# Moving the rotary angles behind the second unit of v, and cutting the last output tile 384 + 128

## The chip, the cores and the metric

The kernel runs on one core of a Trainium2 chip. The metric is the device time of one execution in microseconds (us). The profile is one execution of the same program, taken by the hardware profiler; its engines are TensorE (PE, with its weight loads as PEld), VectorE (DVE), ScalarE (ACT), GpSimd (POOL) and SyncE (SP), which here only issues DMAs.

## The reference, cut to what matters

One encoder layer over 1024 tokens of width 1024. What the change touches is the projection of `a` to v, the angles of the rotary embedding, and the very end (gate, per-layer embedding, final norm):

```python
def rotary(x, positions):
    half = HEAD_DIM // 2
    inv_freq = ROPE_THETA ** (-jnp.arange(half, dtype=jnp.float32) / half)
    ang = positions.astype(jnp.float32)[:, None, :, None] * inv_freq
    cos, sin = jnp.cos(ang), jnp.sin(ang)
...
        a = rms_norm(h, g_mix[i])
        qa, ka, va, qd, kd, vd, gate_na, gate_dil = jnp.split(a @ w_in[i], split_points, axis=-1)
...
        e = rms_norm(h, g_ple[i])
        h = h + jax.nn.sigmoid(e @ w_ple_gate[i]) * (p[i] @ w_ple_proj[i])
    return rms_norm(h, g_final)
```

## The kernel before, in words

Matrices are held as pairs of float32r tiles, a high part and a low part (`split`, lines 106 to 113: ACT casts the high part, DVE or POOL subtracts it to get the low part), and each product is three matmuls (`mm3`, lines 206 to 210, so L208, L209 and L210 in the profile).

**The head.** For eight token tiles of 128 rows (`tt` 0 to 7) the kernel loads x, works out two of the 16 tiles of `p @ W_p` (`ple`), and normalizes and transposes the tile (`norm_to_act`, lines 278 to 282). The norm is a chain of small DVE instructions (L239 to L248) with two DVE instructions at its end that write `xn` (L258). TensorE then transposes `xn` in two halves of four 128x128 blocks (L275) into a PSUM tile `tp`. The pool of `tp` has two buffers, so each half of a tile needs the buffer that the same half of the tile before used. A buffer is free once ACT has cast it (L109, `act10h<-tp`) and DVE has subtracted (L110, `act10l<-tp`). Tiles 4 to 7 go into act10 (first half) and act11 (second half).

Then, in the code, come the rotary angles (lines 340 to 379): four DMAs that broadcast the positions into `pi`, one of `invf`, 20 DVE instructions on 128x256 that reduce the angle modulo 2 pi (L349 to L375, the tiles `a`, `b`, `c`, `d`), two Sin on ACT (L376, L377) and two stores of the tables into DRAM (L379, `cs_scr`). The tables are read back at the start of the q and k stage (L481).

**The v stage.** Five units of v (`v_unit`, line 381, called at line 423). A unit has four PSUM tiles `ps_v` of 48 matmuls with 256 columns, of three buffers (`ps_mm`). Each is cast by ACT and subtracted by DVE into `v_stage`, and stored by four DMAs in the first two units (`v_na`). The weights of a unit are prepared during an earlier unit. Beside it run `left_sums` (line 400), the operand sums of the next stage.

**The end.** For each token tile and each half of 512 columns TensorE multiplies by the gate weights (`ps_t`), ACT takes the sigmoid (L1412), DVE multiplies and adds (L1413, L1415), ACT squares and sums (L1417), and after the second half a chain of small DVE instructions gives the factor with which both halves of the output are scaled. The second half of the last tile is done in two pieces of 256 columns (lines 1430 to 1435), each with 24 matmuls.

**What sets the order.** Every engine takes its instructions in one fixed order. That order is made at build time by a list scheduler with its own model of the times, so instructions of the head and of the v stage are interleaved on each engine, and code that is written elsewhere changes the order around it. DMAs from SP stand in one queue in the same way.

Of the kernel before, what the change touches and what calls it, by code (L numbers as in the profile page):

```python
# [59 lines left out]
def encoder_kernel(ctx: ExitStack, tc: tile.TileContext, t: dict, out: bass.AP):  # L60
# [229 lines left out]
    def dma(dst, src):  # L290
        nc.sync.dma_start(dst.bitcast(F32) if dst.dtype == F32R else dst,
                          src.bitcast(F32) if src.dtype == F32R else src)
# [4 lines left out]
    with ExitStack() as st:  # L297
# [38 lines left out]
                ple(*job)  # L336
            norm_to_act(qp, two(xs[tt]), g, tt, xn=qp.tile([P, D], F32, name="xn", tag="nat"))


        pi = qp.tile([P, 256], I32, name="pi", tag="rt")  # L340
        for a in range(4):
            nc.sync.dma_start(pi[a * 32:(a + 1) * 32],
                              t["positions"][:, a * 256:(a + 1) * 256].broadcast_to((32, 256)))
        invf = qp.tile([P, 1], F32, name="invf", bufs=1)
        nc.sync.dma_start(invf, t["invf"])
        hpi = qp.tile([P, 1], F32, name="hpi", bufs=1)
        nc.vector.memset(hpi, float(np.pi / 2))
        r, k1, k2, ab, sn, cn = (qp.tile([P, 256], F32, name=n_, tag="rt") for n_ in "abcdef")
        nc.vector.tensor_copy(r, pi)  # L349
        nc.vector.tensor_scalar(r, r, invf, None, op0=ALU.mult)  # L350
        big = 4096.0 * TWO_PI
        nc.vector.tensor_scalar(k1, r, 1.0 / big, MAGIC, op0=ALU.mult, op1=ALU.add)
        nc.vector.tensor_scalar(k1, k1, MAGIC, None, op0=ALU.subtract)
        cp = _fixed_parts(big, [2.0 ** (8 - 7 * i) for i in range(8)])
        pp = _fixed_parts(TWO_PI, [2.0 ** (-9 - 12 * i) for i in range(3)])

        def less(k, part, dst=r):
            nc.vector.scalar_tensor_tensor(dst, k, -part, r, op0=ALU.mult, op1=ALU.add)

        for i in range(3):  # L360
            less(k1, cp[i])
        less(k1, cp[3], k2)
        nc.vector.tensor_scalar(k2, k2, 1.0 / TWO_PI, MAGIC, op0=ALU.mult, op1=ALU.add)
        nc.vector.tensor_scalar(k2, k2, MAGIC, None, op0=ALU.subtract)
        less(k2, pp[0])
        less(k1, cp[3])
        less(k2, pp[1])
        less(k1, cp[4])
        less(k1, cp[5])
        less(k2, pp[2])  # L370
        less(k1, cp[6])
        less(k1, cp[7])
        lim = float(np.nextafter(np.float32(np.pi), np.float32(0)))
        nc.vector.tensor_scalar(r, r, lim, -lim, op0=ALU.min, op1=ALU.max)
        nc.vector.scalar_tensor_tensor(ab, r, -1.0, r, op0=ALU.mult, op1=ALU.max)  # L375
        nc.scalar.activation(sn, r, AF.Sin)  # L376
        nc.scalar.activation(cn, ab, AF.Sin, bias=hpi, scale=-1.0)  # L377
        for i, src in enumerate((cn, sn)):
            nc.sync.dma_start(cs_scr[i].rearrange("a f n -> (a f) n"), src)  # L379

        def v_unit(u):
            w2 = take(2, 2)
            for tp_ in range(4):
                ps = ps_mm.tile([P, HALF], F32, name="ps_v", tag="mm")
                pv3 = ps.rearrange("p (a b) -> p a b", a=2)
                for a in range(2):
                    mm_tok(pv3[:, a, :], w2, tp_ * 2 + a)
                stg = qp.tile([P, 2, 4, P], F32R, name="v_stage", tag="nat")
                s4 = ps.rearrange("p (a h d) -> p a h d", a=2, h=4)
                split(stg[:, :, :, 0:64], stg[:, :, :, 64:128], s4)  # L390
                if u < 2:
                    for a in range(2):
                        for r in range(2):
                            dma(v_na[4 * u:4 * u + 4, :, 2 * a + r, tp_, :].rearrange("h c f -> c h f"),
                                stg[r * GW:(r + 1) * GW, a])
                    continue
                dst = v_scr[tp_ * 256:(tp_ + 1) * 256, u * HALF:(u + 1) * HALF]
                dma(dst.rearrange("(a p) c -> p a c", p=P), stg.rearrange("p a h d -> p a (h d)"))

        def left_sums(r):  # L400

# [19 lines left out]
        s1 = []  # L421
        for u in range(5):
            v_unit(u)
            if u < 4:
                s1.append(left_sums(u))
            if u == 0:
                for b in range(2):
                    dma(a_scr[b], flat2(act[1][0][b]))
# [972 lines left out]
    with ExitStack() as st:  # L1401
# [18 lines left out]
        for tt, n in tok_order():  # L1420
            c = slice(n * HALF, (n + 1) * HALF)
            pe = fp.tile([P, HALF], F32, name="pe", tag="pe")
            nc.sync.dma_start(pe, p_scr[tt * P:(tt + 1) * P, c])
            last = tt == NT - 1 and n == 1
            if last:

                hg = fp.tile([P, HALF], F32, name="hg", tag="hg", bufs=1)
                nc.gpsimd.tensor_tensor(hg, h_cols(tt, slice(0, HALF)), g[:, 0:HALF], op=ALU.mult)
                p = parts[tt, 0]
                for a in range(2):  # L1430
                    ps = ps_mm.tile([P, HALF], F32, name="ps_t", tag="mm")[:, :256]
                    mm_tok(ps, w8[4:], tt, slice(a * 256, (a + 1) * 256))
                    q = gated(tt, slice(HALF + a * 256, HALF + (a + 1) * 256), ps, pe[:, a * 256:(a + 1) * 256])
                    if a == 0:
                        nc.vector.tensor_tensor(p, p, q, op=ALU.add)
            else:
                q = gated(tt, c, tok_product(w8, tt, n), pe)
                parts[tt, n] = q
            if n == 1:
                r = rstd_of(fp, (parts[tt, 0], q))  # L1440
                for i in range(2):
                    c = slice(i * HALF, (i + 1) * HALF)
                    o = fp.tile([P, HALF], F32, name="o", tag="o")
# [105 lines left out]
```

## Time and profile before

| | |
|---|---|
| median of 3 runs | 1675.5 us (1675.15, 1675.5, 7496.38) |
| the profiled execution | 1673.03 us, span 1670.8 us |
| TensorE busy | 1571.5 us, 94% of the span |
| VectorE, ScalarE, GpSimd busy | 72%, 42%, 39% of the span |
| mean granted TensorE clock | 0.974 of 2.4 GHz |
| DMA | 279.22 MB, mean 167 GB/s |

A busy TensorE is one with a matmul in its pipeline. Matmuls overlap, so in rows of the timeline the distance from one start to the next is what a matmul costs in a stream, and the second column (its own duration) is longer than that. The granted clock is 1.00 at 2.4 GHz and 0.50 at 1.2 GHz. "[5.32 <-DVE act10l L110]" behind a row says that its engine had been idle for 5.32 us and that this instruction of DVE ended the wait.

### The profile page before, as it was taken

Reading aid. Unit: us, or ns where it says so; the run is one execution under the profiler, and the core shown is the slowest. Engines: PE = TensorE matmul, PEld = TensorE weight load, DVE = VectorE, ACT = ScalarE, POOL = GpSimd, SP = SyncE. Lnnn points to the kernel's source line nnn. Section 1 sums busy time; section 2 is a strip of 40 time slices with the busy share of each in tenths; the row PEclk is TensorE's granted clock in tenths of the full one; section 3 lists DMA queues with packets and bytes.
Section 4 is the critical chain, followed back from the end, with each engine's and each line's share of the span. In section 5 each row is a group of like instructions: output and inputs, shape, how many; then the busy total and the mean of one; then the engine's idle time right before and its main releaser. Section 6 shows DMA issues by size and latency. Waiting matters only on the chain. (4 is left out here: it accounts for less than half of the span.)

```text
span 1670.8 us, 22589 instructions
## 1 busy us (share of the span) xinstructions
PE 1571.5 (94%) x7787; PEld 1312.3 (79%) x7787; DVE 1200.9 (72%) x2081; ACT 708.4 (42%) x1327; POOL 654.0 (39%) x434
## 2 busy tenths in 40 slices
PE   8899999999999998879997899999989999999997
PEld 7899777787787877757886688888877788887886
DVE  6744799734665788645557776777778999999955
ACT  7322222216787666644334333333345333333422
POOL 0233678613333222215304677777742322225100
PEclk9999999999999999989998999999999999999999
DMA  8552455674566778556343344434467454433122
GB/s 309 169 156 103 138 161 160 208 266 165 189 197 217 230 224 275 182 189 183 139 164 126 107 140 139 145 139 146 145 222 277 156 167 161 143 111 128 43 101 70
DMA packets 115058, 279.22 MB, mean 167 GB/s; under 512 B 14240, under 2 KB 30592, under 8 KB 114432
## 3 DMA queue, kind: packets, MB, share of 16 engines
q1 hardware_dynamic: 109184, 267.29, 48.7%
q10 hardware_dynamic: 5760, 10.49, 1.7%
q8 instruction: 62, 1.02, 0.3%
q14 instruction: 52, 0.43, 0.1%
HBM read 186.61 MB, written 91.11 MB: 166 GB/s over the span
## 5 line engine op out<-in xcount | busy, mean ns | idle before, releaser
L109 ACT CAST w_hi<-w_raw 128x512 fp32r<-128x512 f32 (+2 forms) x103 | 83.7, 826 | 144.4 <-POOL w_raw L470 55.9
L110 POOL TENSOR_TENSOR w_lo<-w_raw,w_hi 128x512 fp32r<-128x512 f32 (+2 forms) x33 | 64.2, 1947 | 154.5 <-ACT w_hi L109 150.5
L110 DVE TENSOR_TENSOR f_lo<-f_raw,f_hi 128x512 fp32r<-128x512 f32 x80 | 81.7, 1039 | 52.0 <-ACT f_hi L109 51.3
L110 DVE TENSOR_TENSOR w_lo<-w_raw,w_hi 128x1024 fp32r<-128x1024 f32 (+1 forms) x70 | 85.2, 1224 | 37.7 <-ACT w_hi L109 37.5
L722 POOL TENSOR_SCALAR s_sb<-s_sb,rs 128x384 f32<-128x384 f32 x64 | 41.3, 645 | 134.1 <-DVE rs L721 88.9
L109 ACT CAST f_hi<-f_raw 128x512 fp32r<-128x512 f32 x80 | 46.1, 613 | 82.9 <-DMA f_raw<-w_up 79.7
L110 DVE TENSOR_TENSOR pt_l<-tp_p,pt_h 128x384 fp32r<-128x384 f32 (+3 forms) x120 | 65.0, 543 | 15.4 <-ACT pt_h L109 14.8
L1172 POOL TENSOR_TENSOR u_t<-u_t 128x512 f32<-128x512 f32 x45 | 53.7, 1193 | 38.0 <-ACT u_t L1171 36.8
L109 ACT CAST pt_h<-tp_p 128x384 fp32r<-128x384 f32 (+3 forms) x120 | 56.1, 467 | 24.3 <-PE tp_p L731 14.5
L628 POOL TENSOR_TENSOR k_lo<-k_lo,k_st 128x1024 fp32r<-128x1024 f32 x12 | 33.2, 2767 | 76.1 <-ACT k_st L625 54.4
L1171 ACT ACTIVATE u_t<-u_t 128x512 f32<-128x512 f32 x45 | 28.4, 631 | 74.5 <-DVE u_t L1158 74.1
L1335 DVE TENSOR_TENSOR h<-ps_d,h 128x512 f32<-128x512 f32 x84 | 54.4, 678 | 1.7 <-PE ps_d L210 1.5
L637 PE MATMUL sc<-k_st,q_st 128*128 128x384 f32 (+3 forms) x160 | 53.0, 331 | 0.2 <-DVE stats L655 0.2
L657 ACT ACTIVATE s_sb<-s_sb,stats 128x256 f32<-128x256 f32 (+2 forms) x96 | 44.8, 468 | 19.3 <-DVE stats L655 18.9
L647 ACT ACTIVATE s_sb<-s_sb,nm 128x384 f32<-128x384 f32 x64 | 39.4, 616 | 31.2 <-DVE nm L646 31.0
L110 DVE TENSOR_TENSOR f_lo<-f_t,f_hi 128x512 fp32r<-128x512 f32 x32 | 51.3, 1608 | 1.8
L208 PE MATMUL ps_b<-y_op,w_hi 128*128 128x512 f32 x96 | 39.3, 419 | 11.2 <-ACT y_op L109 8.5
L638 PE MATMUL sc<-k_lo,q_st 128*128 128x384 f32 (+3 forms) x160 | 49.5, 310 | 0.0
L1335 DVE TENSOR_TENSOR sum_t<-ps_d,sum_t 128x512 f32<-128x512 f32 x72 | 46.6, 679 | 2.3 <-PE ps_d L210 2.3
L210 PE MATMUL ps_d<-w_hi,m_op 128*128 128x512 f32 x112 | 43.6, 399 | 2.7 <-DVE m_op L110 2.7
L496 POOL TENSOR_TENSOR o<-x,c 128x512 f32<-128x512 f32 x24 | 40.6, 1707 | 11.2 <-DVE c L491 8.7
L1297 POOL TENSOR_TENSOR t_raw<-pair,w_raw 128x1024 f32<-128x1024 f32 x6 | 15.6, 2598 | 75.0 <-DVE act11l L110 30.8
(478 smaller groups left out, 5826.3 us busy)
## 6 DMA issues: line engine op xcount, KB each, us to landing
f_raw<-w_up SPq DMA_DIRECT2D x32, 512.0 KB
w_raw<-w_in SPq DMA_DIRECT2D x26, 512.0 KB
u_raw<-l_scr SPq DMA_DIRECT2D x25, 512.0 KB
qk_scr<-o SPq DMA_DIRECT2D x96, 128.0 KB
h<-l_scr SPq DMA_DIRECT2D x24, 512.0 KB
l_scr<-u_t SPq DMA_DIRECT2D x42, 256.0 KB
l_scr<-u_s SPq DMA_DIRECT2D x42, 256.0 KB
w_raw<-w_qk SPq DMA_DIRECT2D x20, 512.0 KB
```

What stands on the lines that cost most here:

```text
L109: nc.scalar.copy(hi, src)
L110: eng.tensor_tensor(lo, src, hi.bitcast(F32), op=ALU.subtract)
L208: nc.tensor.matmul(ps, sh, mh, start=first, stop=False)
L210: nc.tensor.matmul(ps, sl, mh, start=False, stop=last)
L496: nc.gpsimd.tensor_tensor(dst, x, y, op=op)
L637: pe(nc.tensor.matmul(o, qs[:, qsl], kk, start=True, stop=False))
L638: pe(nc.tensor.matmul(o, qs[:, qsl], ll, start=False, stop=True))
L647: nc.scalar.activation(s_[:, :n], s_[:, :n], AF.Exp, bias=nm, scale=1.0, accum_out=sm)
L657: nc.scalar.activation(s_[:, :n], s_[:, :n], AF.Exp, bias=nm, scale=-1.0, accum_out=sm)
L722: nc.gpsimd.tensor_scalar(pr, pr, rs, 1.0, op0=ALU.mult, op1=ALU.mult)
L1172: nc.gpsimd.tensor_tensor(c, c, c, op=ALU.mult)
L1335: nc.vector.tensor_tensor(d, ps, d, op=ALU.add)
```

## The change

The block of the angles becomes a function, called after the second unit of v instead of ahead of the first; its instructions are the same. And the last half tile is cut at 384 columns instead of at 256, so that its last piece has 128 columns.

```diff
-        pi = qp.tile([P, 256], I32, name="pi", tag="rt")
-        for a in range(4):
-            nc.sync.dma_start(pi[a * 32:(a + 1) * 32],
-                              t["positions"][:, a * 256:(a + 1) * 256].broadcast_to((32, 256)))
...
+        def angles():
+
+            pi = qp.tile([P, 256], I32, name="pi", tag="rt")
+            for a in range(4):
+                nc.sync.dma_start(pi[a * 32:(a + 1) * 32],
+                                  t["positions"][:, a * 256:(a + 1) * 256].broadcast_to((32, 256)))
...
         for u in range(5):
             v_unit(u)
+            if u == 1:
+                angles()
             if u < 4:
                 s1.append(left_sums(u))
...
-                for a in range(2):
-                    ps = ps_mm.tile([P, HALF], F32, name="ps_t", tag="mm")[:, :256]
-                    mm_tok(ps, w8[4:], tt, slice(a * 256, (a + 1) * 256))
-                    q = gated(tt, slice(HALF + a * 256, HALF + (a + 1) * 256), ps, pe[:, a * 256:(a + 1) * 256])
+                for a, b in ((0, 384), (384, HALF)):
+                    ps = ps_mm.tile([P, HALF], F32, name="ps_t", tag="mm")[:, :b - a]
+                    mm_tok(ps, w8[4:], tt, slice(a, b))
+                    q = gated(tt, slice(HALF + a, HALF + b), ps, pe[:, a:b])
```

**VectorE in the head, before.** From the norm of tile 6 (its `xn` is xn_514) to the subtraction that frees the first `tp` buffer of tile 5 (tp_478); a_613, b_614 and c_615 are tiles of the angles:

```order
L247 SCALAR_TENSOR_TENSOR nw_525<-ny_521,nv_519 128x1
L358 SCALAR_TENSOR_TENSOR a_613<-c_615,a_613 128x256
L243 TENSOR_SCALAR ny_577<-ny_577 128x1
L244 TENSOR_SCALAR nv_575<-nv_575 128x1
L248 SCALAR_TENSOR_TENSOR ny_521<-nw_525,ny_521 128x1
L358 SCALAR_TENSOR_TENSOR a_613<-b_614,a_613 128x256
L247 SCALAR_TENSOR_TENSOR nw_581<-ny_577,nv_575 128x1
L258 SCALAR_TENSOR_TENSOR xn_514<-x_492,ny_521,gain_136 128x512 x2
L358 SCALAR_TENSOR_TENSOR a_613<-c_615,a_613 128x256
L248 SCALAR_TENSOR_TENSOR ny_577<-nw_581,ny_577 128x1
L110 TENSOR_TENSOR act10l_88<-tp_478,act10h_87 128x512
```

The same place in the changed kernel, from the weights' low part w_lo_625 (second piece of the second unit) to the same subtraction:

```order
L110 TENSOR_TENSOR w_lo_625<-w_raw_622,w_hi_624 128x1024
L110 TENSOR_TENSOR act10l_88<-tp_422,act10h_87 128x512
L242 TENSOR_SCALAR ny_577<-nv_575 128x1
L247 SCALAR_TENSOR_TENSOR nw_525<-ny_521,nv_519 128x1
L110 TENSOR_TENSOR act11l_90<-tp_429,act11h_89 128x512
L110 TENSOR_TENSOR v_stage_677<-ps_v_628,v_stage_677 128x8x64
L243 TENSOR_SCALAR ny_577<-ny_577 128x1
L244 TENSOR_SCALAR nv_575<-nv_575 128x1
L248 SCALAR_TENSOR_TENSOR ny_521<-nw_525,ny_521 128x1
L247 SCALAR_TENSOR_TENSOR nw_581<-ny_577,nv_575 128x1
L258 SCALAR_TENSOR_TENSOR xn_514<-x_492,ny_521,gain_136 128x512 x2
L248 SCALAR_TENSOR_TENSOR ny_577<-nw_581,ny_577 128x1
```

The angles are gone from this stretch; the split of the first v tile (v_stage_733 comes next, then act10l_88<-tp_478) and the weights stand in it as before.

**SP's queue, now.** The four loads of `pi` stood between the loads of x for tiles 5 and 7; now they stand behind the stores of the first v tile of the second unit (v_stage_933):

```order
L291 DMA v_na_93<-v_stage_845 64x4x128 x4
L291 DMA v_na_93<-v_stage_933 64x4x128 x4
L362 DMA pi_1108<-positions 32x256 x4
L139 DMA w_raw_1171<-w_in 128x1024
L291 DMA v_na_93<-v_stage_989 64x4x128 x4
```

**VectorE, now, where the angles went.** They are in two runs, ahead of and behind the split of the third v tile of the second unit (v_stage_1045); this is the first run, and the line numbers are those of the changed file (349 became 369, 358 became 378):

```order
L110 TENSOR_TENSOR v_stage_989<-ps_v_940,v_stage_989 128x8x64
L369 CAST a_1117<-pi_1108 128x256
L370 TENSOR_SCALAR a_1117<-a_1117,invf_1113 128x256
L372 TENSOR_SCALAR b_1118<-a_1117 128x256
L373 TENSOR_SCALAR b_1118<-b_1118 128x256
L378 SCALAR_TENSOR_TENSOR a_1117<-b_1118,a_1117 128x256 x3
L378 SCALAR_TENSOR_TENSOR c_1119<-b_1118,a_1117 128x256
L383 TENSOR_SCALAR c_1119<-c_1119 128x256
L384 TENSOR_SCALAR c_1119<-c_1119 128x256
L378 SCALAR_TENSOR_TENSOR a_1117<-c_1119,a_1117 128x256
L110 TENSOR_TENSOR v_stage_1045<-ps_v_996,v_stage_1045 128x8x64
```

All eleven instructions of this run wait for the loads of `pi`, and v_stage_1045 stands behind them.

## Rows read from the trace of the kernel before

**Rows 1.** The page's part 1: busy us, share of the span and instructions of each engine.

```profile
PE 1571.5 (94%) x7787; PEld 1312.3 (79%) x7787; DVE 1200.9 (72%) x2081; ACT 708.4 (42%) x1327; POOL 654.0 (39%) x434
```

**Rows 2.** The waits of TensorE from 0 to 200 us: instruction, what it waited for, us in total, times, longest.

```profile
PE tp L275 <- DVE act10l L110: 5.3, 1, 5.3
PE ps_q L208 <- ACT w_hi L109: 1.2, 1, 1.2
```

**Rows 3.** The timeline of TensorE around the wait: start, duration, instruction, and the idle time before it with its releaser. The first three rows are four transposes and two matmuls of the v stage at full clock.

```profile
41.42 0.60 PE L275 MATMUL tp<-ident,xn 128*128 128x128 f32 x4
41.77 0.36 PE L209 MATMUL ps_v<-w_lo,act01h 128*128 128x256 f32 x1
41.98 0.28 PE L210 MATMUL ps_v<-w_hi,act01l 128*128 128x256 f32 x1
...
50.52 1.28 PE L275 MATMUL tp<-ident,xn 128*128 128x128 f32 x8
51.81 0.39 PE L208 MATMUL ps_v<-w_hi,act10h 128*128 128x256 f32 x1
52.03 0.28 PE L209 MATMUL ps_v<-w_lo,act10h 128*128 128x256 f32 x1
57.63 1.12 PE L275 MATMUL tp<-ident,xn 128*128 128x128 f32 x4 [5.32 <-DVE act10l L110]
58.39 0.56 PE L210 MATMUL ps_v<-w_hi,act10l 128*128 128x256 f32 x1
...
62.17 0.30 PE L208 MATMUL ps_v<-w_hi,act11h 128*128 128x256 f32 x1
```

**Rows 4.** Stretches of the span: busy us and instructions of TensorE, its weight loads, VectorE, ScalarE, GpSimd, then TensorE's granted clock, the DMA share and GB/s.

```profile
52.00:58.00 6.00, 0.68 (x4) 0.48 (x4) 6.00 (x13) 0.42 (x1) 2.49 (x2) 0.78 0.48 110
58.00:62.20 4.20, 4.20 (x22) 4.20 (x21) 3.65 (x12) 0.59 (x2) 0.00 (x0) 0.50 0.00 0
80.00:120.00 40.00, 40.00 (x335) 40.00 (x335) 19.07 (x23) 11.36 (x17) 11.94 (x7) 1.00 0.53 149
```

**Rows 5.** The timeline of VectorE in the head: the first instruction of the angles, the last small ones ahead of the wait's end, and the subtraction that ended it.

```profile
37.99 0.29 DVE L349 CAST a<-pi 128x256 f32<-128x256 int32 x1 [1.05 <-DMA pi<-positions]
...
51.88 1.30 DVE L247 SCALAR_TENSOR_TENSOR nw<-ny,nv 128x1 f32<-128x1 f32 x1
53.10 0.41 DVE L358 SCALAR_TENSOR_TENSOR a<-c,a 128x256 f32<-128x256 f32 x1
53.43 0.14 DVE L243 TENSOR_SCALAR ny<-ny 128x1 int32<-128x1 int32 x1
...
54.09 1.40 DVE L258 SCALAR_TENSOR_TENSOR xn<-x,ny,gain 128x512 f32<-128x512 f32 x2
56.89 0.68 DVE L110 TENSOR_TENSOR act10l<-tp,act10h 128x512 fp32r<-128x512 f32 x1
```

**Rows 6.** Groups of instructions from 0 to 330 us: line, engine, operation, count, busy us, mean ns of one, idle time before. The largest group of the angles on VectorE, and ScalarE's cast of the v tiles.

```profile
L358 DVE SCALAR_TENSOR_TENSOR a<-b,a 128x256 f32<-128x256 f32 x8 | 3.3, 413 | 0.0
L109 ACT CAST v_stage<-ps_v 128x512 fp32r<-128x512 f32 x20 | 11.7, 587 | 44.9 <-PE ps_v L210 44.3 <-ACT w_hi L109 0.6
```

**Rows 7.** The timeline of SP's queue: when DMAs were issued and how long the issuing took.

```profile
34.38 0.43 SPq L342 DMA_DIRECT2D pi<-positions  x1
...
84.74 6.58 SPq L291 DMA_DIRECT2D v_na<-v_stage  x8
```

**Rows 8.** Matmuls in a stream inside the attention stage: two of 384 columns, and four of 128 columns; "128*64" has weights of 64 columns.

```profile
569.08 0.34 PE L637 MATMUL sc<-k_st,q_st 128*128 128x384 f32 x1
569.26 0.34 PE L638 MATMUL sc<-k_lo,q_st 128*128 128x384 f32 x1
...
569.90 0.22 PE L753 MATMUL av<-pt_h,v_t 128*128 128x128 f32 x1
569.96 0.22 PE L754 MATMUL av<-pt_l,v_t 128*64 128x128 f32 x1
570.02 0.27 PE L753 MATMUL av<-pt_h,v_t 128*128 128x128 f32 x1
570.13 0.28 PE L754 MATMUL av<-pt_l,v_t 128*128 128x128 f32 x1
```

**Rows 9.** The timeline of the end: first matmuls of the two pieces and the last of all, and the instructions on ScalarE and VectorE behind them.

```profile
1656.44 0.28 PE L208 MATMUL ps_t<-w_hi,act10h 128*128 128x256 f32 x1
1659.31 0.28 PE L208 MATMUL ps_t<-w_hi,act10h 128*128 128x256 f32 x1
1662.07 0.28 PE L210 MATMUL ps_t<-w_hi,act11l 128*128 128x256 f32 x1
1656.70 0.60 ACT L1412 ACTIVATE sg<-ps_t 128x512 f32<-128x512 f32 x1 [2.63 <-PE ps_t L210]
1658.19 0.69 DVE L1415 TENSOR_TENSOR h<-sg,h 128x512 f32<-128x512 f32 x1
1659.85 0.63 ACT L1417 ACTIVATE sg<-h 128x512 f32<-128x512 f32 x1
1662.45 0.38 ACT L1412 ACTIVATE sg<-ps_t 128x256 f32<-128x256 f32 x1 [0.90 <-PE ps_t L210]
1662.86 0.43 DVE L1413 TENSOR_TENSOR sg<-sg,pe 128x256 f32<-128x256 f32 x1 [1.12 <-ACT sg L1412]
1663.78 0.42 ACT L1417 ACTIVATE sg<-h 128x256 f32<-128x256 f32 x1 [0.95 <-DVE h L1415]
```

More of the change, by code (lines that the diff above doesn't have):

```diff
@@ L337, in encoder_kernel @@
             norm_to_act(qp, two(xs[tt]), g, tt, xn=qp.tile([P, D], F32, name="xn", tag="nat"))
-        pi = qp.tile([P, 256], I32, name="pi", tag="rt")
-        for a in range(4):
-            nc.sync.dma_start(pi[a * 32:(a + 1) * 32],
-                              t["positions"][:, a * 256:(a + 1) * 256].broadcast_to((32, 256)))
[L344 to L379, printed above, removed]
         def v_unit(u):
@@ L398, in v_unit, with less @@
                 dma(dst.rearrange("(a p) c -> p a c", p=P), stg.rearrange("p a h d -> p a (h d)"))
+        def angles():
[3 more added lines that the diff above has]
+                                  t["positions"][:, a * 256:(a + 1) * 256].broadcast_to((32, 256)))
+            invf = qp.tile([P, 1], F32, name="invf", bufs=1)
+            nc.sync.dma_start(invf, t["invf"])
+            hpi = qp.tile([P, 1], F32, name="hpi", bufs=1)
+            nc.vector.memset(hpi, float(np.pi / 2))
+            r, k1, k2, ab, sn, cn = (qp.tile([P, 256], F32, name=n_, tag="rt") for n_ in "abcdef")
+            nc.vector.tensor_copy(r, pi)
+            nc.vector.tensor_scalar(r, r, invf, None, op0=ALU.mult)
+            big = 4096.0 * TWO_PI
+            nc.vector.tensor_scalar(k1, r, 1.0 / big, MAGIC, op0=ALU.mult, op1=ALU.add)
+            nc.vector.tensor_scalar(k1, k1, MAGIC, None, op0=ALU.subtract)
+            cp = _fixed_parts(big, [2.0 ** (8 - 7 * i) for i in range(8)])
+            pp = _fixed_parts(TWO_PI, [2.0 ** (-9 - 12 * i) for i in range(3)])
+            def less(k, part, dst=r):
+                nc.vector.scalar_tensor_tensor(dst, k, -part, r, op0=ALU.mult, op1=ALU.add)
+            for i in range(3):
+                less(k1, cp[i])
+            less(k1, cp[3], k2)
+            nc.vector.tensor_scalar(k2, k2, 1.0 / TWO_PI, MAGIC, op0=ALU.mult, op1=ALU.add)
+            nc.vector.tensor_scalar(k2, k2, MAGIC, None, op0=ALU.subtract)
+            less(k2, pp[0])
+            less(k1, cp[3])
+            less(k2, pp[1])
+            less(k1, cp[4])
+            less(k1, cp[5])
+            less(k2, pp[2])
+            less(k1, cp[6])
+            less(k1, cp[7])
+            lim = float(np.nextafter(np.float32(np.pi), np.float32(0)))
+            nc.vector.tensor_scalar(r, r, lim, -lim, op0=ALU.min, op1=ALU.max)
+            nc.vector.scalar_tensor_tensor(ab, r, -1.0, r, op0=ALU.mult, op1=ALU.max)
+            nc.scalar.activation(sn, r, AF.Sin)
+            nc.scalar.activation(cn, ab, AF.Sin, bias=hpi, scale=-1.0)
+            for i, src in enumerate((cn, sn)):
+                nc.sync.dma_start(cs_scr[i].rearrange("a f n -> (a f) n"), src)
         def left_sums(r):
```

## The prediction

> **What bounds the kernel now.** I read the page first: TensorE is busy for 94% of the span [rows 1], so a change pays only where TensorE stands still or runs slowly. Then the waits of TensorE in the first 200 us [rows 2]: the longest behind the start is one wait of 5.3 us, by transposes for a subtraction of VectorE. The timeline shows it [rows 3]: after the matmul at 52.03 TensorE's next instruction is the transposes of tile 6 at 57.63. They need the PSUM buffer that tile 5's first half holds until `act10l` has read it. On VectorE that subtraction starts only at 56.89 [rows 5], though ScalarE's cast had long been done: VectorE was busy for all 6.00 us from 52 to 58 [rows 4], with angles among the rest. The stretch behind the wait has a price of its own: from 58 to 62.2 us the granted clock is 0.50, that is 1.2 GHz, after TensorE had worked for 0.68 of 6 us; from 80 us on it is 1.00 [rows 4].
>
> At the end nothing but the last piece counts: the matmul at 1662.07 is followed by sigmoid, multiply, add, square and the short norm chain, one after the other [rows 9].
>
> **The change, part by part.** The sum is against the profiled execution, 1673.03 us; its span is 2.2 us shorter and the median of the runs 2.5 us longer than it, so I add the same difference to the median of 1675.5.
>
> *The wait goes.* Thirteen of the 20 angle instructions stood ahead of that `act10l` (L349 to L364 once each but L358 seven times). One of L358 takes 0.41 us [rows 6] and the first, a cast, 0.29, which I take for the other five: 7 x 0.41 + 6 x 0.29 = 4.6 us. Instructions overlap by some 0.08 us (53.10 + 0.41 against 53.43), so they held VectorE for 3.6 to 4.6 us; the first also waited 1.05 us for its positions [rows 5]. Without them `act10l` starts 4.6 to 5.7 us sooner, at 51.2 to 52.3 by subtraction, ends 0.7 us later, and TensorE would want the buffer at about 52.15 (0.12 behind the row at 52.03 [rows 3]; 24 matmuls of 256 columns take 2.87 us at the end, 0.12 each [rows 9]). So up to about 0.9 us of wait is left. Against that, the low part of the next weights now stands ahead of both subtractions of tile 4, and waits for a load; the loads of x for tiles 6 and 7 stand sooner in the queue, as `pi` and `invf` are out of their way. I take 0.5 us of wait left, with bounds of 0 and 3 us. Gain: 5.48 us (52.15 to 57.63) less 0.5 = 5.0 us.
>
> *The slow stretch goes with it.* From 57.63 to 62.17 TensorE did twice four transposes and 13 matmuls of 256 columns. At full clock four transposes and the matmul behind them take 41.98 - 41.42 = 0.56 us, so that work takes 2 x 0.56 + 11 x 0.12 = 2.4 us instead of 4.5 [rows 3]. Gain 2.1 us. The eight transposes at 50.52 took 1.29 us up to the next start where twice 0.35 is the rate (41.42 to 41.77), as the second half of `xn` came late from the same busy VectorE: 0.6 us more, of which I take 0.5. Bounds for both together: 0, if a wait of the same kind stays, and 2.7.
>
> *Where the angles go.* All 20 instructions, at most 20 x 0.41 = 8.3 us, now run on VectorE in the v stage, where it is busy for 19.07 of 40 us while TensorE is busy for all 40 [rows 4]; that spare time hides them. Two Sin and a table load go to ScalarE, which stood idle for 44.9 us ahead of 20 casts of v tiles [rows 6]: nothing. Four loads and two stores move behind stores of v in SP's queue; eight such stores take 6.58 us to issue [rows 7], and what stands behind them is weights for a unit about 23 us later (four tiles of 48 matmuls at 0.12 us): nothing. The new wait is VectorE's for `pi`: four stores (3.3 us) and four loads (1.7 us) after v_stage_933 and then the 3.6 us from the last issue at 34.38 to the first angle at 37.99 [rows 5, 7] make 8.6 us, while VectorE still has three subtractions and the split of a v tile whose matmuls end 5.8 us after those of v_stage_933. So it waits up to 3 us, and then eleven angles (4.5 us at most) stand ahead of v_stage_1045. TensorE needs that PSUM tile's buffer two tiles later, 2 x 5.8 = 11.5 us after it is filled, and cast and subtraction take 1.3 us, so 10 us of delay are free: nothing.
>
> *The last tile.* Matmuls of 384 columns follow each other at 0.18 us [rows 8]. So the first piece takes 24 x 0.175 = 4.2 us instead of 1659.31 - 1656.44 = 2.87: 1.33 us later. For 128 columns with weights of 128 columns the rows show 0.11 (570.02 to 570.13), and 0.06 where the next weights have 64 columns (569.90 to 569.96) [rows 8]. In this product every matmul has new weights of 128 columns, so 0.11: the last matmul starts 23 x 0.11 = 2.53 us after the first of its piece, where it was 2.76. TensorE ends 1.33 - 0.23 = 1.1 us later. Behind it, halving the columns saves 0.105 on the sigmoid (0.60 at 512, 0.38 at 256), 0.13 each on multiply and add (0.69, 0.43), and 0.105 on the square (0.63, 0.42): 0.47 us [rows 9]. Sum: 0.6 us later. Bounds: at 0.12 as with 256 columns 0.9 later; at 0.06 TensorE would end at about 1662.3, but ScalarE, which by its order finishes the square of the first piece before the sigmoid of the second, is free only at about 1663.2 (the first sigmoid at 1660.9, then 0.5 + 0.6 + 0.6 + 0.6 us), and the end is 0.3 later. So no bound is a gain.
>
> The Trainium skill, "TensorE: Matmul & The Clock Gate", section "Back-to-back issue gap", gives a sustained distance of about 81 ns for matmuls of 128 columns. By it the last piece takes 24 x 0.081 = 1.9 us and the end is 0.3 us later, held by ScalarE. This case's rows show 0.11 us, and the sum goes by them.
>
> *Order elsewhere.* A few instructions swap places in the attention and merge stages. None is added there; I put them at 0, give or take 1 us.
>
> *Does the gain reach the end?* From 80 to 120 us TensorE is never idle [rows 4], so the v stage runs at its pace and ends as much sooner as it is ahead there. The next wait is 1.2 us, at the start of q and k, for a cast on ScalarE [rows 2], which itself follows the v stage. I find no event with a time of its own, so all of it passes.
>
> Sum: -5.0 - 2.1 - 0.5 + 0.6 = -7.0 us, 0.4%. **Forecast: 1675.5 - 7.0 = 1668.5 us.**
>
> **The rivals.** *A. The same wait in a new place (0.15).* The low part of the weights waits for its load in front of tile 4's subtractions, or small instructions of VectorE are drawn out again (one took 1.30 us [rows 5]). Then 2 to 4 us of wait and the slow stretch of 2.1 us remain: 7.6 less 4 to 6 is a gain of 1.5 to 3.5, less 0.6 at the end: 1672.5 to 1674.5. For it speaks that VectorE is still the fullest engine there; against, that 3.6 to 4.6 us of work leave it.
>
> *B. The gain is given back later (0.08).* The v stage ends sooner, but a transfer or ScalarE sets the start of a later stage. Then only the tail is left: 1675.5 + 0.6 = 1676.1. Against it: TensorE's waits up to 200 us are all for VectorE and ScalarE, and their work there follows TensorE's.
>
> *C. Slower: the angles stall the v stage (0.05).* If `pi` lands late enough to hold v_stage_1045 by more than 10 us, that is some 5 us later than worked out above, TensorE runs out of PSUM buffers. If then all 20 angles (12 x 0.41 + 8 x 0.29 = 7.2 us, 8.3 at most) and a slow stretch of 2.1 us lie bare, the 7.6 us are more than lost: 1.7 to 2.8 us slower, with the tail 1678 to 1679.
>
> *D. The end alone counts (in A's and B's chances).* If the wait was never on the path, B's time results; the 40 us of busy TensorE behind it speak against that.
>
> **How the numbers follow.** The forecast has 0.72, A 0.15, B 0.08, C 0.05. The forecast's own case runs from 1666.5 (no wait left, 1 us better elsewhere, the low bound at the end) to 1671.5 (a wait of 2 us at full clock, 1 us worse elsewhere, the high bound). The range takes in A as well and stops short of B: 1665 to 1675. 2% is 33.5 us, about what a measurement of this kernel can tell from no change; no case reaches it on either side, and I leave 0.01 for faster and 0.02 for slower by something not seen here. Within 2%: 0.97.
>
> **What would show it.** No wait over 1 us of the transposes for `act10l` before 62 us, and a granted clock of 1.00 from 35 to 120 us; the q and k stage beginning some 7 us sooner; the angles at about 77 to 90 us with TensorE busy throughout; at the end 0.11 us between matmuls of 128 columns, and 6.7 us from the first matmul of the two pieces to the last, where it was 5.6. I am wrong if the transposes still wait, if the stage after v starts no sooner, or if the 128-column matmuls come at 0.06.

## The result, and the profile after

The changed kernel takes 1657.45 us (median of four runs, 1655.12 to 1659.66) where the kernel before takes 1675.33 beside it: a ratio of 0.9909, 95% interval 0.9889 to 0.9928, so 12 to 19 us less, 15.2 by the ratio itself. The two medians are 17.9 us apart; that of before is of four runs, one of which took 7496.38 us. A second measurement of the same kernel, below, gave 0.9915 (0.9899 to 0.9930). The forecast was 1668.5, a gain of 7.0 us: the sign was right, and about twice as much came.

The page's first lines of the changed kernel answer to [rows 1]:

```profile
span 1657.8 us, 22579 instructions
PE 1566.2 (94%) x7787; PEld 1308.7 (79%) x7787; DVE 1197.9 (72%) x2081; ACT 708.7 (43%) x1327; POOL 656.9 (40%) x434
```

**The head.** The waits of TensorE up to 160 us in the changed kernel, beside [rows 2], and the timeline of the transposes that had waited [rows 3]:

```profile
PE ps_p L208 <- ACT w_hi L109: 4.9, 1, 4.9
PE tp L275 <- DVE act10l L110: 1.4, 1, 1.4
```

```profile
53.27 0.66 PE L275 MATMUL tp<-ident,xn 128*128 128x128 f32 x4 [1.43 <-DVE act10l L110]
55.19 0.60 PE L275 MATMUL tp<-ident,xn 128*128 128x128 f32 x4
```

Of the wait of 5.32 us 1.43 are left. The windows of [rows 4] show that the slow clock behind it is gone (the columns behind the engines are granted clock, DMA share, GB/s):

```profile
52.00:58.00 6.00, 4.74 (x40) 4.74 (x41) 5.93 (x12) 1.76 (x3) 1.29 (x1) 1.00 0.55 124
58.00:62.20 4.20, 4.20 (x38) 4.20 (x37) 1.84 (x3) 1.17 (x2) 0.00 (x0) 1.00 0.46 104
80.00:120.00 40.00, 40.00 (x336) 40.00 (x335) 25.02 (x40) 13.57 (x20) 13.30 (x8) 1.00 0.53 158
```

The angles now stand from 78.7 to 89.5 us; VectorE waits 2.2 us for `pi` there, and TensorE is busy for 40.00 of the 40 us. The q and k stage begins 6.4 us sooner: its first matmul, which stood at 163.43 us, now reads

```profile
156.99 0.50 PE L208 MATMUL ps_q<-z2h,w_hi 128*128 128x512 f32 x1 [1.24 <-ACT w_hi L109]
```

**The end.** The rows that answer to [rows 8, 9]: the first matmul of 384 columns, the change to 128 columns, the last matmul, and the first instruction of the norm chain:

```profile
1642.84 0.33 PE L208 MATMUL ps_t<-w_hi,act10h 128*128 128x384 f32 x1
...
1647.02 0.22 PE L208 MATMUL ps_t<-w_hi,act10h 128*128 128x128 f32 x1
1647.08 0.27 PE L209 MATMUL ps_t<-w_lo,act10h 128*128 128x128 f32 x1
1647.19 0.27 PE L210 MATMUL ps_t<-w_hi,act10l 128*128 128x128 f32 x1
...
1649.54 0.28 PE L210 MATMUL ps_t<-w_hi,act11l 128*128 128x128 f32 x1
1651.31 0.21 DVE L239 TENSOR_SCALAR nv<-np 128x1 f32<-128x1 f32 x1 [0.47 <-ACT sg L1420]
```

128 columns come at 0.11 us, and the two pieces take 6.70 us from the first matmul to the last.

**The rest came from places that the change does not name.** I laid the two traces side by side by the same matmul. At 376 us of before the difference is 7.4 us, at 401 it is 10.6. From there to the merge 2.3 us are lost again, the merge gains 4.0 and the long MLP stretch behind it 1.3; the tail costs 0.6, and the spans differ by 13.0. In the attention of the kernel before, ScalarE and TensorE do this:

```profile
386.97 0.48 ACT L109 CAST pt_h<-tp_p 128x384 fp32r<-128x384 f32 x1
387.34 1.07 ACT L624 ACTIVATE q_st<-q_raw 128x1024 fp32r<-128x1024 f32 x1
388.30 1.04 ACT L625 CAST k_st<-k_lo 128x1024 fp32r<-128x1024 f32 x1
389.24 0.51 ACT L657 ACTIVATE s_sb<-s_sb,stats 128x256 f32<-128x256 f32 x1
389.74 1.03 ACT L156 CAST w_hi<-w_raw 128x1024 fp32r<-128x1024 f32 x1
390.67 0.58 ACT L109 CAST pt_h<-tp_p 128x512 fp32r<-128x512 f32 x1
...
391.31 0.39 PE L900 MATMUL av<-pt_h,v_t 128*128 128x256 f32 x1 [2.25 <-ACT pt_h L109]
```

`pt_h` (the high part of the transposed probabilities) of 512 columns stands behind the next head's operands q_st and k_st and the weights' cast w_hi. In the changed kernel it stands ahead of w_hi, and of one exponential:

```profile
378.57 1.06 ACT L627 ACTIVATE q_st<-q_raw 128x1024 fp32r<-128x1024 f32 x1
379.54 1.04 ACT L628 CAST k_st<-k_lo 128x1024 fp32r<-128x1024 f32 x1
...
381.44 0.59 ACT L109 CAST pt_h<-tp_p 128x512 fp32r<-128x512 f32 x1
381.92 0.52 ACT L660 ACTIVATE s_sb<-s_sb,stats 128x256 f32<-128x256 f32 x1
382.42 1.04 ACT L156 CAST w_hi<-w_raw 128x1024 fp32r<-128x1024 f32 x1
...
382.94 0.33 PE L906 MATMUL av<-pt_l,v_t 128*64 128x256 f32 x1 [0.47 <-DVE pt_l L110]
```

A wait of 2.25 us has become one of 0.47. Behind it, the window of before from 393.0 to 396.4 us, and that of the changed kernel from 384 to 390:

```profile
393.00:396.40 3.40, 3.40 (x13) 2.73 (x13) 1.38 (x2) 1.17 (x2) 1.21 (x1) 0.54 0.33 94
```

```profile
384.00:390.00 6.00, 6.00 (x41) 5.29 (x39) 3.68 (x12) 3.96 (x12) 1.93 (x1) 1.00 0.61 231
```

At a granted clock of 0.54 those 3.4 us hold the work of 1.8. In the merge (`ps_b`, the product with the branch weights) a wait is shorter, too, and the slow clock behind it gone: before, one wait of 1.96 us for `gt` and 0.53 behind it; in the changed kernel 1.22 us and 1.00. But no swap stands at this place: from 783 us of before on, ScalarE and VectorE do the same instructions in the same order in both kernels, and ScalarE itself waits for a load of `gt` there (2.97 us before, 3.12 now). The merge's swaps lie 27 to 44 us earlier.

```profile
789.07 0.69 PE L208 MATMUL ps_b<-y_op,w_hi 128*128 128x512 f32 x1 [1.96 <-DVE gt L1058]
789.00:792.40 3.40, 3.33 (x8) 2.67 (x9) 1.90 (x5) 1.68 (x2) 1.28 (x1) 0.53 0.48 154
```

```profile
778.32 0.50 PE L208 MATMUL ps_b<-y_op,w_hi 128*128 128x512 f32 x1 [1.22 <-DVE gt L1061]
778.30:782.00 3.70, 3.68 (x16) 3.07 (x17) 2.18 (x4) 2.13 (x3) 1.29 (x1) 1.00 0.44 142
```

### The profile page after: what moved, and what is told of

The parts are those of the page before. It is cut to its first block, busy times and chain, and to the rows that moved or that the text cites. A ratio compares the mean times of both kernels' runs of the same rounds, so it can differ in the third digit from the quotient of the medians.

```text
span 1657.8 us, 22579 instructions
## 1 busy us (share of the span) xinstructions
PE 1566.2 (94%) x7787; PEld 1308.7 (79%) x7787; DVE 1197.9 (72%) x2081; ACT 708.7 (43%) x1327; POOL 656.9 (40%) x434
## 5 line engine op out<-in xcount | busy, mean ns | idle before, releaser
L109 ACT CAST f_hi<-f_raw 128x512 fp32r<-128x512 f32 x80 | 46.2, 614 | 79.5 <-DMA f_raw<-w_up 74.2
L1174 ACT ACTIVATE u_t<-u_t 128x512 f32<-128x512 f32 x45 | 28.4, 631 | 73.7 <-DVE u_t L1161 73.3
L660 ACT ACTIVATE s_sb<-s_sb,stats 128x256 f32<-128x256 f32 (+2 forms) x96 | 44.8, 468 | 18.8 <-DVE stats L658 18.4
```

What stands on the lines that cost most here:

```text
L109: nc.scalar.copy(hi, src)
L660: nc.scalar.activation(s_[:, :n], s_[:, :n], AF.Exp, bias=nm, scale=-1.0, accum_out=sm)
```

## The experiments

The theory (O, for order): the surplus comes from the swaps that the list scheduler made behind the v stage. The rivals: it comes from the 128 columns (T), or from meeting DMAs and the clock 7 us sooner, whatever the order (S).

**The two edits apart, and the angles elsewhere.** `head_only` puts the last tile back to 2 x 256 columns, `tail_only` puts the angles back; `u0` calls the angles behind the first unit, `u2` (with `u == 2`) behind the third:

```diff
-            if u == 1:
+            if u == 0:
                 angles()
```

> The angles behind the second unit of v, the last half tile still in 2 x 256 columns. Theory O (order): besides the 7.4 us of the head, the change gains about 6 us because the list scheduler also orders the attention and the merge otherwise; the last tile costs 0.6. Then this kernel is 0.6 us faster than the changed kernel: 17 to 19 us faster than before where the changed kernel is 15 to 18 faster. Theory T (tail): the 128 columns bring the surplus; then this one is only 7 to 8 us faster than before.

> The angles where they were, the last half tile cut 384 + 128. The order of every engine is that of before but for the last tile. Theory O: 0.6 us slower than before (0.3 to 0.9). Theory T: 6 to 9 us faster.

> The angles behind the first unit of v instead of the second, the last tile as in the change. Behind the v stage DVE, ACT, POOL and SP have exactly the order of before (but for the last tile), not that of the change. Theory O: the gain is that of the head alone, 6 to 8 us less 0.6: 5.5 to 7.5 us faster than before, with the waits of before at 388 us (2.2 us, av for pt_h) and at 787 us (2.0 us, ps_b for gt) and the slow clock behind each. Rival S (shift): what is 7 us sooner meets DMAs and the clock otherwise, whatever the order: then as fast as the changed kernel, 15 to 18 us faster than before. If the angles bar the head again, less gain, and the wait stands before 75 us.

> The angles behind the third unit of v, the last tile as in the change. TensorE's order is that of the change throughout, and the attention and the merge have the change's order on every engine. Theories O and S both: as the changed kernel, 15 to 18 us faster than before, within 1 us of it; the first 75 us as there, since no angle stands in the head in either.

Measured: `head_only` 0.9934 (0.9911 to 0.9957), 11 us faster; `tail_only` 1.0003 (0.9989 to 1.0017); `u0` 1.0006 (0.9994 to 1.0019); `u2` 0.9939 (0.9920 to 0.9957), 10 us faster. The tail brings nothing, so T falls. The two kernels with the change's order gain 10 to 11, where 15 to 19 were expected; that is more than a head's 7, but the lower ends of both intervals are at 7. `u0` tells less than it was meant to: the scheduler put its angles into the head again, and the transposes waited there as before, now in two waits:

```profile
PE tp L275 <- DVE act10l L110: 3.8, 1, 3.8
PE tp L275 <- DVE xn L258: 1.5, 1, 1.5
```

So it could not tell O from S.

**One order or the other.** The scheduler's order behind the v stage can be tipped by edits that cost nothing. `change_again` is the changed kernel. `a_q5` and `b_q3` call the second head's operands a tile later or sooner (5 in the changed kernel, 3 in the kernel before):

```diff
-            if qi == 4:
+            if qi == (5 if h == 8 else 4):
                 ready_ops.append(operands(h + 1 if h < 19 else 0))
```

and `b_merge` adds to the kernel before

```diff
         qo = st.enter_context(tc.tile_pool(name="qk_out", bufs=1, reuse_waits="tile"))
+        dmy = wp.tile([P, 64], F32, name="dmy", tag="dmy")
+        for _ in range(1):
+            tc.keep_in_program_order(nc.gpsimd.memset(dmy, 0.0))
```

> The changed kernel itself once more, beside the three that follow, since single executions differ by several us. Theory O by the parts of the profiles: head and start of q and k 7.3, attention 3, merge 1.5 to 3.3, last tile 0.6 lost: 11 to 13 us faster than before. If the first comparison (15 to 18) was typical, something is still missing in that sum.

> The changed kernel, with the operands of the second head of the dilated attention called one tile later in the code (at its sixth tile instead of the fifth). That gives DVE, ACT and SP nearly the order of before in the attention (the cast w_hi ahead of pt_h of 512 columns again, q_st two tiles later) and exactly that of before in the merge; the head is that of the change. Theory O: the gain of the head alone is left, 7.3 less 0.6: 5.5 to 7.5 us faster than before, 4 to 6 slower than the changed kernel, with the wait of av for pt_h at the start of the attention back at about 2 us. Rival S (what comes 7 us sooner meets DMAs and the clock otherwise, whatever the order): as fast as the changed kernel.

> The kernel before, with one memset of 128x64 on POOL at the start of the q and k stage. That is enough for the scheduler to give the merge (and one swap ahead of it) exactly the change's order; head and attention stay as before. Theory O: 1.5 to 3.3 us faster than before, with no wait of ps_b for gt of 2 us at 787. Rival S: as before, within 0.7.

> The kernel before, with the operands of the second head of the dilated attention called one tile sooner in the code (at its fourth tile). q_st and k_st stand two to four rows sooner on ACT and DVE, and the merge has the change's order; the head stays as before. Theory O: the attention's 3 us (if the wait of av for pt_h goes, as with the change) and the merge's 1.5 to 3.3: 4 to 6 us faster than before. Rival S: as before, within 0.7.

Measured: `change_again` 0.9915 (0.9899 to 0.9930), 14.2 us faster; `a_q5` 0.9971 (0.9960 to 0.9983), 3 to 7 us faster; `b_merge` 1.0002 (0.9991 to 1.0012); `b_q3` 0.9988 (0.9977 to 0.9999). `a_q5` has the changed head and nearly the old order; the wait for `pt_h` is back, and the surplus is gone: S falls.

```profile
383.83 0.39 PE L903 MATMUL av<-pt_h,v_t 128*128 128x256 f32 x1 [2.60 <-ACT pt_h L109]
```

`b_merge` missed: its merge stage was 5 us shorter than that of before in the trace, and nothing of it reached the end. In that trace 3.8 of the 5 us go in the MLP, from the merge to the end's first `ps_t`: 766.0 us at a granted clock of 0.97, where before has 762.2 at 0.98. `b_q3` missed in the attention: with q_st sooner, a new wait of equal length took the old one's place, so the edit did not undo what it was to undo:

```profile
PE tp_p L860 <- DVE pt_l L110: 2.5, 1, 2.5
```

**The attention alone, with the changed head.** `a_attn` adds the memset of `b_merge` to the changed kernel; `a_both` adds instead, ahead of the attention,

```diff
+        for _ in range(3):
+            tc.keep_in_program_order(nc.scalar.activation(stats[2], ident[:, 0:64].rearrange('p (a b c) -> p a b c', a=2, b=4), AF.Copy))
```

> The changed kernel with one memset of 128x64 on POOL at the start of the q and k stage. Its order differs from the change's in one place alone: at the start of the attention ACT's cast pt_h of 512 columns stands behind the exponential and the cast w_hi, as before the change, and DVE's q_st two rows later. Head, merge and tail are those of the change. Theory O (each swap is worth what its stage shows): the stretch 380 to 400 of before lasts 20 to 21 us instead of 17, and the kernel is 3 to 4 us slower than the change: 10 to 11 us faster than before. Theory S: as the change, 14 us faster. Theory M (the attention is worth nothing at the end, as the merge seems to be, and something else separates the change from the kernel with the old order): also 14.

> The changed kernel with three copies of 128x64 on ACT ahead of the attention (some 0.2 us each, on an engine that is idle there). That swaps the attention as in the kernel before this one, and gives the merge the order of before the change as well. Theory O: 3 to 4 us lost in the attention and about 3 in the merge: 7 to 8 us faster than before, or, if the merge is worth nothing at the end, 10 to 11. If the second head's operands one tile later (3.7 us faster than before) cost something of their own, this one is clearly faster than that; if the order is all, both are within 2 us of each other. Theory S: 14 us faster.

Measured: `a_attn` 0.9939 (0.9922 to 0.9956), 10.2 us faster than before; `a_both` 0.9958 (0.9945 to 0.9972), 7.0 faster. These are O's totals (10 to 11, and 7 to 8), but the stages do not bear out how O came by them. The start of the attention is only 1.2 to 1.4 us longer in `a_attn` than in the two traces of the changed kernel, where 3 to 4 were expected, and of the 3.2 us between the two kernels the merge shows 1.2. And `u2`, which has the change's order, gained 10.2 as well. So that this one swap is worth 4 us at the end is not shown, and M is not ruled out by it. What is clear is this: with the changed head and the old order `a_q5` gains 4.9 us (3 to 7), and every measurement of the change's order 10.2 to 15.2, with intervals above that of `a_q5`. In `a_attn` one swap of `pt_h` brings the wait back:

```profile
383.11 1.04 ACT L156 CAST w_hi<-w_raw 128x1024 fp32r<-128x1024 f32 x1
384.05 0.59 ACT L109 CAST pt_h<-tp_p 128x512 fp32r<-128x512 f32 x1
...
384.68 0.39 PE L906 MATMUL av<-pt_h,v_t 128*128 128x256 f32 x1 [1.49 <-ACT pt_h L109]
```

**The same pattern where it stands again.** In the changed kernel it comes once more, as the second measurement's trace shows:

```profile
410.72 1.05 ACT L156 CAST w_hi<-w_raw 128x1024 fp32r<-128x1024 f32 x1
411.67 1.06 ACT L627 ACTIVATE q_st<-q_raw 128x1024 fp32r<-128x1024 f32 x1
412.62 1.03 ACT L628 CAST k_st<-k_lo 128x1024 fp32r<-128x1024 f32 x1
413.56 0.59 ACT L109 CAST pt_h<-tp_p 128x512 fp32r<-128x512 f32 x1
...
414.20 0.39 PE L903 MATMUL av<-pt_h,v_t 128*128 128x256 f32 x1 [1.69 <-ACT pt_h L109]
416.06 0.33 PE L906 MATMUL av<-pt_l,v_t 128*64 128x256 f32 x1 [1.48 <-DVE pt_l L110]
```

The next edits to the changed kernel are all of one kind: at which tile of a head the next head's operands are called. Heads are numbered from 8 here, so `{10: 2}` is the third head, which calls those of the fourth: `{9: 2}` in `a_h9_2`, `{9: 6}` in `a_h9_6`, `{10: 6}` in `a_h10_6`, `{10: 2}` in `a_h10_2`, `{9: 2, 10: 6, 11: 2}` in `a_mix`, `{10: 2, 12: 2}` in `a_h10_2_h12_2`, `{9: 2, 10: 2, 12: 2}` in `a_best`.

```diff
-            if qi == 4:
+            if qi == {10: 2}.get(h, 4):
```

> The changed kernel, with the operands of the third head of the dilated attention called at the third tile of the second head instead of the fifth. In the changed kernel's trace the pattern of the old attention stands a second time, 26 us later: w_hi, q_st and k_st (3.1 us of ACT) ahead of pt_h of 512 columns, q_st ahead of pt_l on DVE; TensorE waits 1.69 and 1.48 us there, and a slow stretch follows. With this edit q_st and k_st stand six rows sooner on ACT, and pt_h no longer behind them; head, merge, MLP and tail as in the change. Theory O: both waits fall to under 1 us, and 2 to 4.5 us are gained over the change: 16 to 19 us faster than before. Rival Q: q_st waits for its load there and holds ACT, or the next head's pieces collide: a wait of another place takes over, and the time is that of the change, 14 faster.

> The same, with the operands of the third head two tiles later instead of sooner (at the seventh tile): q_st and k_st behind pt_h of 512 columns on ACT, q_st behind pt_l on DVE. Theory O: the waits of 1.69 and 1.48 us fall to under 1 us here too, 2 to 4.5 us gained over the change: 16 to 19 us faster than before. Rival Q: the low part k_lo (3.3 us on POOL, behind k_st) is late for the third head's first score some 10 us later; then a wait of sc for k_lo of 1 to 3 us takes over, and the time is that of the change.

Measured: 0.9902 (0.9883 to 0.9922) and 0.9915 (0.9897 to 0.9933). Both missed their place: head 9's call is the one 14 us ahead of the waits, which stayed at 1.69 and 1.49 us. That `a_h9_2` lies within O's 16 to 19 us (16.4) is luck, then. It shortened the place that it hit by 1.2 us; in `a_h9_6` rival Q's wait for `k_lo` came, 1.46 us.

> The changed kernel, with the operands of the fourth head of the dilated attention called two tiles later. That is the place (412 to 416 us in the trace of the changed kernel) where w_hi, q_st and k_st stand ahead of pt_h of 512 columns on ACT and q_st (2.5 us) ahead of pt_l on DVE; the two runs with the third head had hit the place before it. Here pt_h comes behind w_hi alone and pt_l ahead of q_st; merge and all else as in the change. Theory O: the waits of 1.69 and 1.48 us fall to under 0.7 each and 2 to 4 us are gained: 16 to 18 us faster than before. Rival Q: k_lo of that head is late for its first score, as it was for the third head (1.46 us), and gives 1 to 2 of it back.

> The same, two tiles sooner: q_st and k_st before both, pt_h of 512 columns ahead of w_hi. But this edit also gives the merge the order of before the change. So it tells what the merge's order is worth at the end: if nothing (as the kernel before with the change's merge showed), 17 to 19 us faster than before; if 3 to 4 (as the pair of changed kernels with swapped attention showed), 13 to 15.

> A version meant to beat both: the changed kernel with the operands of the third and fifth head called two tiles sooner (the third was worth 1.2 us in its stage) and those of the fourth two tiles later; merge in the change's order. Theory O: the third's 1.2 us and the fourth's 2 to 4 us, 17 to 20 us faster than before. Rival Q: new waits at the fifth head eat that; as the change, 14.

Measured: `a_h10_6` 0.9909 (0.9891 to 0.9927), 15 us faster; `a_h10_2` 0.9895 (0.9871 to 0.9918), 17.6 faster, the fastest of all medians at 1655.54 us; `a_mix` 0.9899 (0.9879 to 0.9919), 17 faster. In `a_h10_6` the two waits fell to 0.59 us together, and Q's came:

```profile
418.44 0.36 PE L641 MATMUL sc<-k_lo,q_st 128*128 128x192 f32 x1 [1.85 <-POOL k_lo L631]
```

In `a_h10_2` one wait of 0.75 us is left of them, and the clock stays up:

```profile
412.02 0.30 PE L863 MATMUL tp_p<-ident,s_sb 128*128 128x128 f32 x1 [0.75 <-DVE pt_l L110]
412.00:422.00 10.00, 9.98 (x63) 8.40 (x64) 5.36 (x17) 6.95 (x21) 2.39 (x1) 1.00 0.59 220
```

> The kernel with the fourth head's operands two tiles sooner (18.4 us faster than before, merge in the old order), and the sixth head's two tiles sooner as well; no wait stood at the sixth head, so this adds nothing there, but it gives the merge the change's order. The merge stage is 77 to 79 us instead of 79.75. If the merge's order is worth its stage's 2.4 us at the end: 19 to 22 us faster than before. If it is worth nothing at the end: 18 to 19.

> A version meant to beat both kernels: that of the run before, and the third head's operands two tiles sooner, too (worth 1.2 us in its stage). 19 to 22 us faster than before, 1652 to 1655 us beside a before of 1674, if the parts add up; as the change, 14, if the time that they free is given back in the slow stretches of later stages.

Measured: 0.9901 (0.9885 to 0.9918) and 0.9914 (0.9898 to 0.9930), 16.6 and 14.4 us faster. Neither adds up. The sixth head's operands, sooner, made a wait where none had stood, again with a q_st (2.40 us) ahead of `pt_l` on VectorE:

```profile
441.04 0.40 PE L920 MATMUL tp_s<-ident,stats 128*64 128x128 f32 x1 [2.59 <-DVE pt_l L110]
```

No version is clearly ahead of the changed kernel: the intervals of `a_h10_2` and `change_again` overlap.

**All profiled executions by stage**, in us between the same matmuls in every trace: the head up to the first matmul of `ps_q`; the start of the attention, from the first `sc` to the `av` that stands at 400.97 in before; from there to the first `ps_b`; the merge up to the first `ps_t`; and the end, from the first `ps_t` behind the MLP to the last instruction. "Old" and "new" are the order of before and of the change; "part" is the change's with the one swap of `pt_h`. Two stretches are left out: the q and k stage, 217.6 to 219.3 us in every kernel, and the MLP, 759.1 to 763.3 us in all but `b_merge`.

| kernel | attention, merge | head | start of attention | to merge | merge | end |
|---|---|---|---|---|---|---|
| before | old, old | 163.4 | 19.1 | 330.7 | 78.2 | 98.8 |
| tail_only | old, old | 164.5 | 20.2 | 331.3 | 77.7 | 99.4 |
| u0 | old, old | 163.5 | 22.1 | 332.9 | 76.2 | 99.4 |
| b_merge | old, new | 164.6 | 18.8 | 331.6 | 73.2 | 98.8 |
| b_q3 | other, new | 163.8 | 20.1 | 330.6 | 75.7 | 98.8 |
| a_q5 | old, old | 155.7 | 19.5 | 331.8 | 78.7 | 99.4 |
| a_both | part, old | 156.3 | 18.8 | 332.3 | 76.5 | 99.4 |
| a_attn | part, new | 157.5 | 17.2 | 331.7 | 75.3 | 99.4 |
| change | new, new | 157.0 | 15.8 | 333.0 | 74.2 | 99.4 |
| change_again | new, new | 157.5 | 16.0 | 328.7 | 74.2 | 99.4 |
| head_only | new, new | 156.7 | 15.8 | 334.5 | 74.9 | 98.8 |
| u2 | new, new | 158.0 | 17.4 | 331.1 | 76.8 | 99.4 |
| a_h9_2 | new, new | 155.9 | 15.8 | 329.8 | 73.3 | 99.4 |
| a_h9_6 | new, new | 158.4 | 15.8 | 331.3 | 75.9 | 99.4 |
| a_h10_6 | new, new | 156.5 | 16.7 | 329.7 | 76.0 | 99.4 |
| a_h10_2 | new, old | 156.8 | 16.4 | 326.5 | 76.1 | 99.4 |
| a_mix | new, new | 156.3 | 17.6 | 327.5 | 77.2 | 99.4 |
| a_h10_2_h12_2 | new, new | 158.8 | 16.5 | 327.8 | 75.4 | 99.4 |
| a_best | new, new | 157.6 | 15.8 | 329.0 | 75.9 | 99.4 |

Means: the head 164.0 with the angles in it and 157.1 without, 6.9 us. The start of the attention 19.9 in the five old, and 16.3 in the four traces whose order there is the change's in every row (`change`, `change_again`, `head_only`, `u2`): 3.7 us. The merge 77.2 in six old and 75.2 in thirteen new: 2.0 us. The end 0.6 longer. Sum: -12.0 us. The four measurements with the change's order and none of the later edits gained 15.2, 14.2, 11.0 and 10.2 us, 12.7 in the mean. Two traces of the same order differ by up to 6 us in the stretch "to merge", so the 0.7 between 12.0 and 12.7 tell nothing. That spread goes with the clock: the longest, 334.5 us in `head_only`, has a granted clock of 0.95 there, and the 328.7 us of `change_again` 0.97. As an estimate, 5% and 3% of these stretches are 17 and 10 us short of full speed.

**How much of it is order.** In the attention order sets the wait: it is 2.25 to 2.60 us in the five traces with the old order, 0.47 in the four of the change's. The slow clock behind it goes along less strictly. It stands in all five of the old; of the four it stands in one, `u2`, whose start of the attention is 1.6 us longer for it:

```profile
384.01 0.33 PE L906 MATMUL av<-pt_l,v_t 128*64 128x256 f32 x1 [0.47 <-DVE pt_l L110]
384.00:388.00 4.00, 3.99 (x14) 3.25 (x15) 0.68 (x1) 2.62 (x7) 2.59 (x2) 0.59 0.77 273
```

In the merge order does not even set the wait: `u2` has the change's order on every engine there, and waits for `gt` about as long as before (1.96 us), with a merge of 76.8 us:

```profile
780.10 0.50 PE L208 MATMUL ps_b<-y_op,w_hi 128*128 128x512 f32 x1 [1.93 <-DVE gt L1061]
```

So the merge's 2.0 us are a mean that goes with the new order; that the swaps make it is not shown.

## Why the prediction was wrong

**The head: right in the sum.** Forecast 7.6 us (5.0 for the wait, 2.1 and 0.5 for the slow stretch), 6.9 measured. The term that was off is the wait left over, put at 0.5 with bounds of 0 and 3: it was 1.43, so the sign "no wait over 1 us" did not come, and one of the signs of being wrong, that the transposes still wait, did. The clock came as forecast, 1.00 from 52 to 62 us, and the q and k stage began 6.4 us sooner for "some 7".

**The angles: right.** VectorE's wait for `pi` was 2.2 us of the "up to 3", and TensorE did not feel it. But `u0` shows that their new place is only good because it lies far enough behind: one unit sooner they are back in the head.

**The last tile: right to 0.02 us.** Forecast 0.6, measured 99.36 - 98.77 = 0.59; TensorE 1.07 later for 1.1, and 0.48 back behind it for 0.47. The distance of matmuls of 128 columns was 0.11 us, as the rows of before had it; the 81 ns of the Trainium skill ("TensorE: Matmul & The Clock Gate", section "Back-to-back issue gap") are not reached here; by the estimate from them the end would have been 0.3 us later.

**"Does the gain reach the end?": right, within what the runs can tell.** The two kernels with the changed head and the old order, `a_q5` and, but for part of the attention, `a_both`, gain 4.9 and 7.0 us at the end, where the head less the tail is 6.3.

**"Order elsewhere": this step failed.** It said that a few instructions swap places in the attention and the merge, that none is added there, "I put them at 0, give or take 1 us". In the attention they took the wait for `pt_h` from 2.25 to 0.47 us and, mostly, the slow clock behind it away: 3.7 us in the mean of its stage. The merge came out 2.0 us shorter in the mean, without its order being shown as the reason. That none is added was true and beside the point: a swap is a move, and it was not priced as the step of the head was. The rows to do it with were in the trace of before: `av` waiting 2.25 us for `pt_h`, and the swapped w_hi of 1.03 us as the instruction that ScalarE did just ahead of it, with 1.6 us lost to the slow clock behind (3.4 us at 0.54). At the bottom of the range, too, 1 us better elsewhere was all that was allowed for; with -3.7 and -2.0 the same sum gives 1675.5 - 7.0 - 5.7 = 1662.8 us. The ratios of the two measurements put the changed kernel at 1660 to 1661, and its first median was 1657.45; the rest is not explained.

Of the rivals none came: not A (the wait that remains keeps the clock up), not B, not C. A mechanism of the side that came, a further gain by the scheduler's order, was not among them.

**What stays open.** What the merge's order is worth, in its stage and at the end. The stage is 2.0 us shorter in the mean, but not in `u2`; the kernel before with the new merge gained nothing (1.5 us faster to 2.0 slower), `a_attn` is 3 us ahead of `a_both`, and `a_h10_2` is the fastest with the old one. Open, too, is why kernels with the change's order gained from 10.2 to 15.2 us: their intervals overlap, and their traces differ in the clock.

## What to carry to other kernels

Where a list scheduler sets the order, a code move is two changes: the one that is meant, and the swaps hundreds of us behind it. Compare the whole order of every engine, and price each swap by the wait that stands at that place in the trace: who waits for the instruction that moved past. And look for casts that TensorE waits for standing behind work for a later head: here one memset of 128x64 was enough to bring back a wait that the change had removed. A shorter stage in one trace is not yet a gain: `b_merge` had 5 us of it, and none at the end.

## What the runs showed of the hardware

A wait of TensorE may cost more than itself. Behind those of 2.25 and 1.96 us the windows above read 0.54 and 0.53 for 3.4 us, nearly all of it at the lower level of 1.2 GHz, and 1.6 us are lost in each. Nor does the length of the one wait decide it: in `a_attn` and in `a_both` the same wait for `pt_h` lasted 1.49 us, and the windows behind it read 1.00 and 0.72, while `u2` above has 0.59 behind one of 0.47:

```profile
385.00:390.00 5.00, 4.66 (x29) 3.91 (x29) 2.29 (x6) 2.36 (x9) 1.61 (x1) 1.00 0.80 302
```

```profile
386.00:392.00 6.00, 6.00 (x28) 5.10 (x27) 2.81 (x8) 2.74 (x8) 0.00 (x0) 0.72 0.37 137
```

As an estimate, about half of the change's gain is clock: over the timed runs of `change_again` the mean granted clock is 0.9777, in those of before beside it 0.9731: 37 of 1658 us short of full speed, against 45 of 1672, which is 8 of the 14.2 us.

VectorE can be drawn out beside GpSimd. q_st takes 1.22 us on VectorE in most heads; in the fourth head of the changed kernel (`change_again`), with two subtractions of GpSimd beside it, it took 2.52, and `pt_l` behind it came so much later. Its start is 412.76, but it ends 1.07 us behind the end of w_lo (414.21), about as if it had begun there; k_lo, which came next, took 3.34 us. In before the same pair reads 2.54 and 3.35 us, and the twelve k_lo on GpSimd go from 2.44 to 3.35. The Trainium skill ("SBUF — State Buffer", section "Who interferes with whom") has a VectorE instruction with two inputs in SBUF contend with a GpSimd instruction that reads SBUF, one waiting for the whole of the other, and these rows agree to some 0.2 us:

```profile
411.85 2.36 POOL L157 TENSOR_TENSOR w_lo<-w_raw,w_hi 128x1024 fp32r<-128x1024 f32 x1 [11.31 <-ACT w_hi L156]
412.76 2.52 DVE L630 SCALAR_TENSOR_TENSOR q_st<-q_raw,q_st 64x1024 fp32r<-64x1024 f32 x1
414.16 3.34 POOL L631 TENSOR_TENSOR k_lo<-k_lo,k_st 128x1024 fp32r<-128x1024 f32 x1
```
